# A decoder trunk on one core: 26 weight slots instead of 24, small inputs laid out by the host, and all weights as one array of whole tiles

## The chip, the cores and the metric

The kernel runs on one core of one Trainium2 chip. The metric is the device time of one execution in microseconds (us); lower is better. Three runs of the kernel before took 1004.30, 1004.28 and 1002.66 us (median 1004.28).

## What is computed

Two layers over 256 tokens of width 1024, all in float32. Each layer is a token mixer with a layer norm behind it, then a mixture of experts (MoE) with a layer norm behind it.

```python
for l in range(2):
    parts = split(x @ w_in[l])                       # 3944 columns
    o_a, o_b, o_c = mla(parts), dilated(parts), sparse(parts)
    g = sigmoid(x @ w_gate[l] + b_gate[l])           # 3 branches x 1024
    merged = g[0] * (o_a @ w_a[l]) + g[1] * (o_b @ w_b[l]) + g[2] * (o_c @ w_c[l])
    x = layer_norm(alpha * x + merged @ w_o[l], ln1_g[l], ln1_b[l])
    # one expert group of four per token, then two of its eight experts
    y = sum(combine[:, e:e+1] * ((silu(x @ w1[l][e]) * (x @ w3[l][e])) @ w2[l][e]) for e in range(32))
    x = layer_norm(alpha * x + y, ln2_g[l], ln2_b[l])
```

Each expert has three 1 MB matrices, so the 32 experts of a layer are 96 tiles of 1 MB; the mixer of a layer has 40 tiles, most of them 1 MB.

## The kernel before

**Slots.** SBUF holds NSLOT = 24 slots of 8 KB per partition (1 MB each). Activations and weights share them (class `Slots`). The class `Ring` holds the 272 weight tiles of both layers in the order of their use. `get` hands a tile to the code that uses it, `done` gives its slot back, and at every change of the count `pump` issues as many further tiles as fit: `fits` looks at the log of a dry run of the same program, so that a prefetched tile never takes a slot that an activation needs before the tile is done. Every weight load is issued on SP's queue (`issue`, lines 191 to 198), in the order of the list. Before a load is started, SP waits until the slot's last reader is done; it also waits for the load eight places before it.

**Layout of the weights.** `plan_weights` (L347) cuts the weights into tiles. A whole expert's w1, w3 or w2 lies in HBM as one run of 1 MB, 8 KB per partition. The other tiles are cut out of wider matrices: chunks of w_in with 408 to 512 columns (rows of about 1.6 to 2 KB), gate tiles with 256 columns (rows of 1 KB). In each MoE three kinds of tiles are cut so that work can start before a whole expert is there: w1 of experts 0 to 3 and w3 of experts 28 to 31 by pieces of k (`by_k`; four transfers of 256 KB a tile, rows of 2 KB), and w2 of experts 28 to 31 by columns (512, 256, 256; rows of 2 and 1 KB).

**Small inputs.** `load_small` (L402) fills 59 rows of a 128x128 tile (gains and biases), the router's weights and its bias with eleven transfers on POOL's queue. It runs in `setup` for layer 0 and at the end of the third group of four experts (`e == 2 * Q`) for layer 1. `load_gains` (L448) fetches the two rows of the last norm on POOL's queue in the sixth group (`e == NE - 3 * Q`), and `mixer` fetches `gpk` there too.

**Stages.** `setup` loads x and the first chunks, `make_xT` transposes x (L522). The mixer of a layer is written out by hand in the order of PE. `moe` (L1690 on) takes the experts in eight groups of four: w1 and w3 (both L1708), the gather of the next group (L1667), w2 (L1788), and the combination of the group before (L1774). A group needs twelve tiles, which come in the order w1, w1, w3, w3, w2, w2 of two experts, then the same of the other two:

```python
w = [self.ring.get((l, n, e + i)) for i in range(Q)]
for k in range(KD):
    up(c, k, [w[i][:, k] for i in range(Q)])
```

So the first product of a group waits for the eighth of its twelve tiles. The last group (experts 28 to 31) comes in another order: four w1, four pieces of w3, then w2 by columns. Between its pieces stand short dummy products (`warm`, L294). `spread_gains` (L461) spreads the rows of the last norm in the seventh group.

## Time and profile before

| what | value |
|---|---|
| three runs, median | 1004.28 us |
| the profiled execution | 1004.42 us |
| its span (first to last instruction) | 1002.7 us |
| PE busy | 902.2 us, 90% |
| DVE, ACT, POOL busy | 473.8, 419.0, 165.6 us |
| moved by DMA | 284.76 MB, mean 284 GB/s |
| mean granted clock of PE | 0.954 |

The profiled execution lies 1.7 us above its span and 0.14 us above the median of the runs. Its page gives each engine's busy time; the span in 40 slices of 25 us with each engine's share in tenths, the clock that PE was granted, and the load of the 16 DMA engines; and the chain of waits that ended last. A busy share of 90% is a mean over stages, so the same quantities are then read stretch by stretch.

### The profile page before, as it was taken

What the parts mean: (1) busy time and instruction counts of PE and PEld (TensorE: products, weight loads), DVE (VectorE), ACT (ScalarE), POOL (GpSimd) and SP (SyncE); (2) the same over time, 40 slices, a digit from 0 to 9 for tenths busy, and PEclk for the clock granted to TensorE, in tenths of its full rate; (3) what the DMA queues carried; (4) which work ended last, traced back from release to release, by engine and by line L of the source; (5) the groups of instructions that cost most, each with busy time, mean ns of one, the idle gap of its engine ahead of it and who ended that gap; (6) DMA issues with size and microseconds to landing.
All of it is one profiled execution on the core that took longest, in us unless ns stands there. A gap on an engine that the chain in (4) does not pass through costs nothing.

```text
span 1002.7 us, 18677 instructions
## 1 busy us (share of the span) xinstructions
PE 902.2 (90%) x7584; PEld 706.5 (70%) x7591; DVE 473.8 (47%) x968; ACT 419.0 (42%) x911; POOL 165.6 (17%) x278
## 2 busy tenths in 40 slices
PE   8999999999999966769999999999999997776694
PEld 7888899999985633435489888998999754443251
DVE  5848676945553111111288687676566421100014
ACT  5545555644552301122274646665444632220131
POOL 4531110012100210000035162000451000000001
PEclk9999999999999977789999999999999999987798
DMA  9933171597879999999994044436959899999994
GB/s 330 324 123 126 44 251 43 169 344 244 336 256 404 415 401 419 418 417 396 357 383 139 19 136 149 138 109 217 329 205 401 305 416 417 421 417 419 419 354 150
DMA packets 100170, 284.76 MB, mean 284 GB/s; under 512 B 6324, under 2 KB 53808, under 8 KB 78576
## 3 DMA queue, kind: packets, MB, share of 16 engines
q1 hardware_dynamic: 99088, 283.12, 75.0%
q8 instruction: 62, 1.02, 0.4%
q0 software_dynamic: 992, 0.39, 0.2%
q14 instruction: 28, 0.23, 0.1%
HBM read 282.44 MB, written 1.05 MB: 283 GB/s over the span
## 4 chain that ended last, share of the span: by engine, by line
PE 57%; DMA 25%; issue 8%; POOL 3%; DVE 3%; ACT 2%; SPq 1%; POOLq 0%; DVEq 0%; ACTq 0%
DMA w<-in_w_dram 23%; PE bank L286 12%; PE bank L287 12%; PE bank L288 12%; PE bank L1708 5%; PE bank L840 3%; DMA w<-in_w_in_dram 2%; PE bank L894 2%; PE bank L881 2%; PE bank L1788 2%; PE bank L1667 2%; DVE ws L282 1%; PE bank L843 1%; ACT xp L1443 1%; PE bank L1774 1%
## 5 line engine op out<-in xcount | busy, mean ns | idle before, releaser
L282 DVE TENSOR_TENSOR ws<-w,ws 128x1024 fp32r<-128x1024 f32 (+2 forms) x154 | 190.8, 1248 | 128.3 <-ACT ws L281 123.4
L1708 PE MATMUL bank<-w,xg 128*32 128x256 f32 x2048 | 148.5, 423 | 69.0 <-DMA w<-in_w_dram 59.8
L1708 PEld LDWEIGHTS bank<-w,xg 128*32 128x32 f32 x2048 | 71.0, 121 | 148.3 <-DMA w<-in_w_dram 70.8
L281 ACT ACTIVATE ws<-w 128x1024 fp32r<-128x1024 f32 (+2 forms) x158 | 158.6, 1023 | 35.2 <-PE bank L288 14.4
L286 PE MATMUL bank<-ws,xTh 128*128 128x408 f32 (+3 forms) x320 | 115.9, 362 | 1.2 <-ACT xTh L281 1.2
L286 PE MATMUL bank<-xTh,ws 128*128 128x256 f32 x384 | 111.2, 290 | 0.0
L287 PE MATMUL bank<-ws,xTh 128*128 128x408 f32 (+3 forms) x320 | 110.0, 344 | 1.1 <-POOL ws L282 1.1
L288 PE MATMUL bank<-ws,xTl 128*128 128x408 f32 (+3 forms) x320 | 110.2, 344 | 0.1
L287 PE MATMUL bank<-xTl,ws 128*128 128x256 f32 x384 | 108.6, 283 | 0.0
L288 PE MATMUL bank<-xTh,ws 128*128 128x256 f32 x384 | 108.5, 283 | 0.0
L1738 DVE SCALAR_TENSOR_TENSOR t<-t,cw,bank 128x256 f32<-128x256 f32 x16 | 10.8, 676 | 199.8 <-PE bank L1708 199.8
L1671 ACT ACTIVATE xg<-bank,gpk 128x128 f32<-128x128 f32 x128 | 50.9, 454 | 95.3 <-PE bank L1667 92.7
L286 PEld LDWEIGHTS bank<-xTh,ws 128*128 128x128 f32 x384 | 73.5, 191 | 1.8 <-issue 1.0
L287 PEld LDWEIGHTS bank<-xTl,ws 128*128 128x128 f32 x384 | 73.6, 192 | 0.2
L288 PEld LDWEIGHTS bank<-xTh,ws 128*128 128x128 f32 x384 | 73.5, 191 | 0.0
L1733 ACT ACTIVATE t<-bank 128x256 f32<-128x256 f32 x16 | 6.1, 384 | 146.3 <-PE bank L1708 146.3
L856 ACT ACTIVATE p<-bank,nb 128x128 f32<-128x128 f32 (+1 forms) x92 | 37.3, 420 | 70.0 <-DVE nb L848 65.1
L286 PEld LDWEIGHTS bank<-ws,xTh 128*128 128x128 f32 x320 | 60.9, 190 | 7.7 <-issue 1.7
L1667 PE MATMUL bank<-xg,xp 128*128 128x128 f32 x512 | 63.0, 276 | 2.0 <-ACT xg L1671 2.0
L1667 PEld LDWEIGHTS bank<-xg,xp 128*128 128x128 f32 x512 | 60.6, 192 | 5.9 <-issue 2.5
L287 PEld LDWEIGHTS bank<-ws,xTh 128*128 128x128 f32 x320 | 60.9, 190 | 4.7 <-POOL ws L282 1.4
L288 PEld LDWEIGHTS bank<-ws,xTl 128*128 128x128 f32 x320 | 60.8, 190 | 4.9 <-DVE xTl L282 0.7
(361 smaller groups left out, 1582.2 us busy)
## 6 DMA issues: line engine op xcount, KB each, us to landing
w<-in_w_dram SPq DMA_DIRECT2D x168, 1024.0 KB, 19.0
w<-in_w_gate_dram SPq DMA_DIRECT2D x24, 1024.0 KB, 5.4
w<-in_w_dram SPq DMA_DIRECT2D x80, 256.0 KB, 7.2
w<-in_w_in_dram SPq DMA_DIRECT2D x18, 1024.0 KB, 11.8
w<-in_w_in_dram SPq DMA_DIRECT2D x12, 816.0 KB, 12.8
w<-in_w_o_dram SPq DMA_DIRECT2D x8, 1024.0 KB, 10.0
w<-in_w_a_dram SPq DMA_DIRECT2D x4, 1024.0 KB, 5.4
w<-in_w_c_dram SPq DMA_DIRECT2D x4, 1024.0 KB, 5.3
```

Source lines behind the costliest of these rows:

```text
L281: self.nc.scalar.activation(hi, src, AF.Copy)
L282: (self.nc.gpsimd if self.lo_pool else self.nc.vector).tensor_tensor(lo, src, hi.bitcast(F32), op=ALU.subtract)
L286: m(out, sh, mh, start=start, stop=False)
L287: m(out, sh, ml, start=False, stop=False)
L288: m(out, sl, mh, start=False, stop=stop)
L840: nc.tensor.matmul(b[:, j * w:(j + 1) * w], q[:, blk * P:(blk + 1) * P], k[:, 0:w], start=j == 0, stop=False)
L856: nc.scalar.activation(p[:, j], v[:, j], AF.Exp, bias=nb[:, j:j + 1], scale=u["scale"], accum_out=sm[:, j:j + 1])
L881: nc.tensor.transpose(ps[:, n * P:(n + 1) * P], p[:, j * P:(j + 1) * P], self.ident)
L894: nc.tensor.matmul(ps[half * 64:(half + 1) * 64, pr * P:(pr + 1) * P], u["v"](u["heads"][pr], kb), u["pt"][:, u["pt0"] + pr * nkb + kb], s ...
L1667: nc.tensor.matmul(ps[:, i * P:(i + 1) * P], self.xn[:, t, k + i], pm[:, t, j:j + Q].rearrange("p e c -> p (e c)"), start=t == 0, stop=t = ...
L1671: nc.scalar.activation(xg[:, k + i], ps[:, i * P:(i + 1) * P], AF.Identity, bias=b, scale=g)
L1708: nc.tensor.matmul(hp[i * CAP:(i + 1) * CAP, c * 256:(c + 1) * 256], xg[:, k, i * CAP:(i + 1) * CAP], w[i], start=k == 0, stop=k == KD - 1 ...
```

## The change

- NSLOT goes from 24 to 26. To make room the kernel asks for 64 bytes of scratch for the DMAs that POOL issues, and POOL issues none any more.
- The host writes all 272 weight tiles one behind the other into one array, `stream`, each tile as it lies in SBUF: partition by partition, each partition's bytes in one run of up to 8 KB. Every tile is one transfer. The order of the tiles is the same. w1, w3 and w2 stay as inputs for a path for overfull experts.
- The host lays out the small inputs: `vecs` (128 rows of 128 values, and the router's bias in row 0), `router` and `gpk`. `load_small` makes two transfers in place of eleven, on ACT's queue in `setup` and on SP's queue in the MoE. `gpk` and the rows of the last norm go to SP's queue, one transfer each.
- The rows of the last norm are loaded in the fourth group (`e == 3 * Q`), not in the sixth.

```diff
-NSLOT = 24
+NSLOT = 26
...
+def tiles(l):
...
+    def kp(a, n):
+        return a.reshape(n, P, -1).transpose(1, 0, 2)
...
+    def by_k(n, e0):
+        for k in range(0, KD, 2):
+            yield (l, n, e0, k), [P, Q, 2, DE], lambda a, k=k: np.stack([pk(a[n][l, e], KD)[:, k:k + 2] for e in range(e0, e0 + Q)], 1)
...
+def laid_stream(a):
+    out = np.empty(NSTREAM, np.float32)
+    o = 0
+    for l in range(L):
+        for _, shape, view in tiles(l):
+            n = P * int(np.prod(shape[1:]))
+            out[o:o + n].reshape(shape)[...] = view(a)
+            o += n
+    return out
...
         key, shape, src = self.queue.pop(0)
         t = self.slots.tile(shape, F32, "w")
-        for i, part in enumerate(src if isinstance(src, list) else ()):
-            self.nc.sync.dma_start(t[:, i], part)
-        if not isinstance(src, list):
-            self.nc.sync.dma_start(t, src)
+        self.nc.sync.dma_start(t, src)
...
     def plan_weights(self, l):
...
+        for key, shape, o, n in STREAM:
+            if key[0] == l:
+                src = self.a["stream"][o:o + P * n]
...
+                self.ring.add(key, shape, src.rearrange(pat, p=P, **kw))
...
     def load_small(self, l, home, o):
...
-        v = self.v = self.t([P, P], F32, "vec", 1)
-        nc.gpsimd.memset(v, 0.0)
-        nc.gpsimd.dma_start(v[0:2], a["q_norm_g"][l].rearrange("(k p) -> k p", p=P))
...
-        nc.gpsimd.dma_start(self.wgb[:, :, 40:72], a["w_sub"][l].rearrange("(k p) f -> p k f", p=P))
...
+        eng = nc.sync if l else nc.scalar
+        small = self.t([P, P + 36], F32, "vec", 1)
+        eng.dma_start(small, a["vecs"][l])
+        self.v, self.br = small[:, 0:P], small[0:1, P:P + 36]
         self.wgs = home
...
+        eng.dma_start(home[:, o + KD * 36:o + 2 * KD * 36], a["router"][l])
...
-    def load_gains(self, l, which, rows=P):
+    def load_gains(self, l):
         gb = self.slots.alloc([P, 2, D], F32, "gb")
-        for j, n in enumerate(("g", "b")):
-            self.nc.gpsimd.dma_start(gb[:rows, j], self.a[f"ln{which}_{n}"][l:l + 1].broadcast_to([rows, D]))
+        self.nc.sync.dma_start(gb[:1], self.a["ln2"][l:l + 1])
...
                 self.gpk = self.t([P, 2 * KD], F32, "gpk", 1)
-                for j, n in enumerate(("ln1_g", "ln1_b")):
-                    nc.gpsimd.dma_start(self.gpk[:, j * KD:(j + 1) * KD], self.a[n][l].rearrange("(p k) -> p k", p=P))
+                nc.sync.dma_start(self.gpk, self.a["gpk"][l])
...
-            if e == NE - 3 * Q:
-                self.gb2 = self.load_gains(l, 2, 1)
+            if e == 3 * Q:
+                self.gb2 = self.load_gains(l)
...
-    nc = _bacc.Bacc("TRN2", target_bir_lowering=False, num_devices=1)
+    nc = _bacc.Bacc("TRN2", target_bir_lowering=False, num_devices=1, dynamic_dma_scratch_size=64)
```

The order of PE and DVE is the same in both kernels but for the name of one operand. It differs on the queues, at three places.

**ACT's queue at the start of the program** (`vec` holds gains and biases, `masks` is the slot in which the router's weights wait). Before:

```order
L1361 ACT_TABLE_LOAD
L1361 ACTIVATE dummy_122<-one 128x1
L281 ACTIVATE xTh_124<-bank_126 128x4x128
L281 ACTIVATE xTh_124<-bank_133 128x4x128
L281 ACTIVATE ws_147<-w_84 128x832
```

Now:

```order
L444 DMA vec_108<-in_vecs_dram 128x164
L448 DMA masks_103<-in_router_dram 128x288
L1387 ACT_TABLE_LOAD
L1387 ACTIVATE dummy_111<-one 128x1
L364 ACTIVATE xTh_113<-bank_115 128x4x128
```

The two small loads of layer 0 now stand ahead of ACT's first work; before, POOL issued eleven at that point.

**SP's queue at the start of the mixer of layer 0**, where the first load stands that waits for another engine (DVE, PE) to give a slot back; DMAHW names are the waits for the load eight places before. Before:

```order
L197 DMA w_163<-in_w_in_dram 128x4x408 [waits DMAHW6_49]
L197 DMA w_165<-in_w_in_dram 128x4x512 [waits DMAHW7_49]
L197 DMA w_167<-in_w_in_dram 128x4x512 [waits DMAHW0_49]
L197 DMA w_169<-in_w_in_dram 128x8x256 [waits DMAHW1_49]
L197 DMA w_225<-in_w_in_dram 128x4x512 [waits DMAHW2_49,DVE_49,PE_49]
L197 DMA w_268<-in_w_in_dram 128x4x512 [waits DMAHW3_49,DVE_49]
```

Now:

```order
L280 DMA w_152<-in_stream_dram 128x1632 [waits DMAHW0_49]
L280 DMA w_154<-in_stream_dram 128x2048 [waits DMAHW1_49]
L280 DMA w_156<-in_stream_dram 128x2048 [waits DMAHW2_49]
L280 DMA w_158<-in_stream_dram 128x2048 [waits DMAHW3_49]
L280 DMA w_160<-in_stream_dram 128x2048 [waits DMAHW4_49]
L280 DMA w_162<-in_stream_dram 128x2048 [waits DMAHW5_49]
L280 DMA w_218<-in_stream_dram 128x2048 [waits DMAHW6_49,DVE_49,PE_49]
L280 DMA w_261<-in_stream_dram 128x2048 [waits DMAHW7_49,DVE_49]
```

w_163 and w_152 are the same tile, the tenth. Two more tiles go out ahead of the first that waits for a slot, and the load that waits is the 16th tile instead of the 14th.

**SP's queue in the MoE of layer 0**, where the small loads of layer 1 now stand; `wr` is a slot, the `w` are weight tiles. Before, SP has weight tiles alone there, and POOL has twelve rows, of which these are the first:

```order
L405 MEMSET vec_3908 128x128
L406 DMA vec_3908<-in_q_norm_g_dram 2x128
L407 DMA vec_3908<-in_kv_norm_g_dram 1x16x8
L408 DMA vec_3908<-in_b_gate_dram 24x128
L409 DMA vec_3908<-in_ln_g_dram 8x128
```

Now SP has:

```order
L280 DMA w_3883<-in_stream_dram 128x2048
L280 DMA w_3885<-in_stream_dram 128x2048
L444 DMA vec_3888<-in_vecs_dram 128x164
L448 DMA wr_3887<-in_router_dram 128x288
L280 DMA w_3924<-in_stream_dram 128x2048
L280 DMA w_3926<-in_stream_dram 128x2048
```

The two loads moved from POOL's queue into the row of the weights on SP's. w_3885 is the 97th tile of the layer; the fifth group, whose end uses what `load_small` brought, takes tiles 89 to 100. The rows of the last norm stand in the same way behind the 108th tile.

## Rows read from the trace of the kernel before

**Rows 1.** The page: the span in 40 slices of 25 us.

```profile
PE   8999999999999966769999999999999997776694
PEclk9999999999999977789999999999999999987798
DMA  9933171597879999999994044436959899999994
GB/s 330 324 123 126 44 251 43 169 344 244 336 256 404 415 401 419 418 417 396 357 383 139 19 136 149 138 109 217 329 205 401 305 416 417 421 417 419 419 354 150
```

**Rows 2.** Chain of waits: start us, us, what; both MoE stages.

```profile
321.80 15.23 DMA w<-in_w_dram
337.09 19.88 DMA w<-in_w_dram
...
439.85 12.45 DMA w<-in_w_dram
452.34 5.36 PE bank L1708 x58
...
815.81 16.73 DMA w<-in_w_dram
...
892.44 20.24 DMA w<-in_w_dram
```

**Rows 3.** Timeline of PE, fourth to seventh group of layer 1: start, us, [idle before <-releaser].

```profile
852.53 4.93 PE L1708 MATMUL bank<-w,xg 128*32 128x256 f32 x58 [1.44 <-DMA w<-in_w_dram]
...
942.76 5.88 PE L1708 MATMUL bank<-w,xg 128*32 128x256 f32 x58 [1.43 <-DMA w<-in_w_dram]
949.12 3.66 PE L1708 MATMUL bank<-w,xg 128*32 128x256 f32 x64 [0.47 <-ACT t L1733]
```

**Rows 4.** Stretches: PE, PEld, DVE, ACT, POOL busy; PE's clock, DMA share, GB/s.

```profile
240.00:255.00 15.00, 15.00 (x127) 15.00 (x126) 8.92 (x14) 7.94 (x12) 3.07 (x4) 1.00 0.44 150
735.00:745.00 10.00, 10.00 (x85) 10.00 (x85) 7.39 (x6) 4.66 (x7) 9.20 (x6) 1.00 0.09 38
790.00:795.00 5.00, 4.51 (x71) 2.47 (x69) 0.70 (x2) 3.48 (x9) 0.68 (x2) 1.00 0.42 102
795.00:943.00 148.00, 110.77 (x1170) 63.60 (x1174) 24.03 (x40) 31.86 (x82) 4.82 (x8) 0.89 1.01 418
940.00:945.00 5.00, 3.30 (x26) 1.28 (x30) 0.00 (x0) 0.00 (x0) 0.00 (x0) 0.50 1.01 419
```

**Rows 5.** Layer 1, fourth group: PE's wait for its seventh tile.

```profile
850.03 1.06 PE L1708 MATMUL bank<-w,xg 128*32 128x256 f32 x2 [4.58 <-DMA w<-in_w_dram]
```

**Rows 6.** SP's queue, 300 to 452 us: waited for, us in total, times, longest.

```profile
SPq L197 <- DMA w<-in_w_dram: 94.1, 45, 3.7
SPq L197 <- PE bank L1708: 14.3, 6, 5.8
```

**Rows 7.** Stretches of DMA at the end of layer 1.

```profile
970.00:978.00 8.00, 7.84 (x81) 3.45 (x81) 0.00 (x0) 1.57 (x3) 0.00 (x0) 1.00 1.00 348
979.00:984.00 5.00, 4.14 (x18) 0.66 (x16) 0.42 (x1) 0.00 (x0) 0.00 (x0) 1.00 1.09 351
```

**Rows 8.** Timeline of PE, last group of layer 0: w2 by columns.

```profile
490.48 1.92 PE L1788 MATMUL bank<-w,t 128*32 128x512 f32 x16 [0.52 <-DVE t L275]
492.33 0.60 PE L294 MATMUL bank<-mk 128*128 128x512 bf16 x2
492.87 1.07 PE L1788 MATMUL bank<-w,t 128*32 128x256 f32 x16
...
496.61 1.39 PE L1774 MATMUL bank<-y,t 128*128 128x256 f32 x8
```

**Rows 9.** The same of layer 1.

```profile
979.76 2.12 PE L1788 MATMUL bank<-w,t 128*32 128x512 f32 x6 [0.52 <-DVE t L275]
982.20 1.90 PE L1788 MATMUL bank<-w,t 128*32 128x512 f32 x10 [0.32 <-DMA w<-in_w_dram]
...
989.34 1.36 PE L1774 MATMUL bank<-y,t 128*128 128x256 f32 x8
```

**Rows 10.** Start of the program: timeline of PE and of ACT, and two stretches.

```profile
5.62 1.06 PE L522 MATMUL bank<-cst,x 128*128 128x128 f32 x8 [0.80 <-DMA x<-in_x_dram]
9.44 1.09 PE L522 MATMUL bank<-cst,x 128*128 128x128 f32 x8 [1.89 <-DMA x<-in_x_dram]
...
6.28 1.08 ACT L281 ACTIVATE xTh<-bank 128x512 fp32r<-128x512 f32 x2 [4.02 <-PE bank L522]
...
10.00:12.00 2.00, 2.00 (x14) 1.98 (x13) 1.97 (x3) 1.09 (x2) 0.00 (x0) 1.00 1.06 208
12.00:25.00 13.00, 13.00 (x71) 12.68 (x70) 8.72 (x9) 7.96 (x11) 3.28 (x5) 1.00 1.05 387
```

**Rows 11.** Layer 0: a stretch; PE behind the spread gains in layers 0 and 1.

```profile
355.00:360.00 5.00, 1.06 (x2) 0.18 (x2) 0.00 (x0) 0.00 (x0) 0.41 (x1) 0.68 1.04 338
...
477.00:478.00 1.00, 1.00 (x14) 0.43 (x8) 0.00 (x0) 0.00 (x0) 0.00 (x0) 0.50 0.93 342
475.00 5.35 PE L1708 MATMUL bank<-w,xg 128*32 128x256 f32 x64
...
965.97 3.66 PE L1708 MATMUL bank<-w,xg 128*32 128x256 f32 x64
```

More of the change, by code (lines that the diff above doesn't have):

```diff
@@ new lines, in stream @@
+def stream():
+    o, out = 0, []
+    for l in range(L):
+        for key, shape, _ in tiles(l):
+            n = int(np.prod(shape[1:]))
+            out.append((key, shape, o, n))
+            o += P * n
+    return out, o
+STREAM, NSTREAM = stream()
+def laid_stream(a):
+    out = np.empty(NSTREAM, np.float32)
+    o = 0
+    for l in range(L):
+        for _, shape, view in tiles(l):
[3 more added lines that the diff above has]
+    return out
@@ L347, in plan_weights @@
     def plan_weights(self, l):
-        a, r = self.a, self.ring
-        kp = "(k p) f -> p k f"
-        def win(c):
-            _, c0, w = CHUNKS[c]
-            if w > 256:
-                for h in range(2):
-                    r.add((l, "in", c, h), [P, 4, w], a["w_in"][l, h * 512:(h + 1) * 512, c0:c0 + w].rearrange(kp, p=P))
-            else:
-                r.add((l, "in", c, 0), [P, 8, w], a["w_in"][l, :, c0:c0 + w].rearrange(kp, p=P))
-        for c in range(3):
-            win(c)
@@ L374, in plan_weights @@
-        for h in range(2):
-            r.add((l, "w_o", 0, h), [P, 4, 512], a["w_o"][l, h * 512:(h + 1) * 512, 0:512].rearrange(kp, p=P))
-        for c in (1, 2):
-            c0, w = WO[c]
-            r.add((l, "w_o", c), [P, 8, w], a["w_o"][l, :, c0:c0 + w].rearrange(kp, p=P))
-        pk = "(p k) f -> p k f"
-        def by_k(n, e0):
-            for k in range(0, KD, 2):
-                r.add((l, n, e0, k), [P, Q, 2, DE], [a[n][l, e].rearrange(pk, p=P)[:, k:k + 2] for e in range(e0, e0 + Q)])
@@ L385, in plan_weights @@
-        by_k("w1", 0)
-        for e in range(0, NE - Q, 2):
-            for n in ("w1", "w3") if e >= Q else ("w3",):
-                for i in range(2):
-                    r.add((l, n, e + i), [P, 8, DE], a[n][l, e + i].rearrange(pk, p=P))
-            for i in range(2):
-                r.add((l, "w2", e + i), [P, 2, D], a["w2"][l, e + i].rearrange("(p j) f -> p j f", p=P))
-        for e in range(NE - Q, NE):
-            r.add((l, "w1", e), [P, 8, DE], a["w1"][l, e].rearrange(pk, p=P))
@@ L394, in plan_weights @@
[L394 to L399 removed]
+        for key, shape, o, n in STREAM:
+            if key[0] == l:
+                src = self.a["stream"][o:o + P * n]
+                pat = "(p a) -> p a" if len(shape) == 2 else f"(p {' '.join('abc'[:len(shape) - 1])}) -> p {' '.join('abc'[:len(shape) - 1])}"
+                kw = {c: d for c, d in zip("abc", shape[1:])} if len(shape) > 2 else {}
+                self.ring.add(key, shape, src.rearrange(pat, p=P, **kw))
@@ L442, in small_rows @@
         for k in range(KD):
-            nc.tensor.matmul(ps[:, 0:72], self.one.broadcast_to([P, P]), self.wgb[:, k], start=k == 0, stop=False)
+            nc.tensor.matmul(ps[:, 0:72], self.one.broadcast_to([P, P]), self.wgb[:, :, k], start=k == 0, stop=False)
         nc.tensor.matmul(ps[:, 36:72], self.one[0:1].broadcast_to([1, P]), self.br, start=False, stop=True)
@@ L1939, with laid_out @@
     Trunk(tc, ctx, a, out, dbg, (dry.slots.log, dry.ring.ends)).run()
-_INS = ["x", "w_in", "q_norm_g", "w_uq", "kv_norm_g", "w_ukv", "w_gate", "b_gate", "w_a", "w_b", "w_c", "w_o",
-        "ln1_g", "ln1_b", "w_group", "b_group", "w_sub", "b_sub", "w1", "w3", "w2", "ln2_g", "ln2_b"]
+_INS = ["x", "w1", "w3", "w2"]
+def laid_out(a):
+    vecs = np.zeros((L, P, P + 36), np.float32)
+    for l in range(L):
+        m = max(l - 1, 0)
+        rows = [a["q_norm_g"][l], a["kv_norm_g"][l], a["b_gate"][l], a["ln1_g"][l], a["ln1_b"][l], a["ln2_g"][m], a["ln2_b"][m]]
+        v = np.concatenate([r.reshape(-1, P) for r in rows])
+        vecs[l, :len(v), :P] = v
+        vecs[l, 0, P:P + 4], vecs[l, 0, P + 4:] = a["b_group"][l], a["b_sub"][l]
+    router = np.concatenate([a["w_group"], a["w_sub"]], 2).reshape(L, KD, P, 36).transpose(0, 2, 1, 3).reshape(L, P, KD * 36)
+    gpk = np.concatenate([a[n].reshape(L, P, KD) for n in ("ln1_g", "ln1_b")], 2)
+    return {"vecs": vecs, "router": router, "gpk": gpk, "ln2": np.stack([a["ln2_g"], a["ln2_b"]], 1)}
 def kernel(**inputs):
```

89 lines of the change are left out of this document (53 added, 36 removed).

## The prediction, made before the changed kernel ran

> **What bounds the kernel now.** Read the 40 slices first [rows 1]. In both mixers (slices 3 to 8 and 22 to 28 above all) PE stands at 9 while the DMA line has low digits: PE sets the time and the weights come with room to spare. In the MoEs (slices 15 to 18 and 34 to 38) it is the other way: DMA at 9 and 401 to 419 GB/s, PE at 6 and 7, its clock line mostly at 7 and 8. The chain of waits says the same: from 321.80 us to 452.34 in layer 0 and from 815.81 to 912.7 in layer 1 it runs through weight loads, and behind that through PE [rows 2].
>
> The timeline of PE shows how such a wait looks. The first product of a group waits for the eighth of the group's twelve tiles. Between the same point of the fourth and the seventh group of layer 1 lie 942.76 - 852.53 = 90.23 us and 36 tiles: **2.51 us a tile of 1 MB**, the 418 GB/s that the stretch has at a DMA share of 1.01 [rows 3, 4]. PE needs less for a group, so until the seventh group its pace doesn't matter: what counts is how far the loads are ahead when the DMA engines become busy for good, at about 300 and 795 us. Just before, they idle: share 0.42 from 790 to 795, 0.09 from 735 to 745, 0.44 from 240 to 255 [rows 4]. There the loads wait for slots, not for bandwidth. From 452.34 and 942.76 on PE works without a long wait to the end of the MoE; that is the seventh group's rest and the eighth.
>
> **The change part by part.** All sums are against the profiled execution, 1004.42 us; the runs' median is 0.14 lower.
>
> *Two slots.* The order on SP's queue shows that two more tiles go out before the first that waits for a slot, and the tile numbers stay shifted by two into the MoE. The idle DMA time can carry them: 10 us at 0.09 leave 9.1, 15 us at 0.44 leave 8.4, and two tiles need 5.0 [rows 4]. So when the DMA engines become busy for good, they are two tiles further, and the eighth tile of the seventh group lands 2 x 2.51 = 5.0 us earlier. PE is there in time: it waited 4.58 us and 1.44 more already in the fourth group of layer 1 [rows 3, 5], so 5.0 leave about 1 us of that wait; the loads stay in front there, and the wait in the seventh group moves by the full 5.0. **Minus 5.0 us in each layer, minus 10.0.** Bounds: 8 (some of a wait turns into PE's own pace) and 10.2.
>
> *The early rows of the last norm* hold a slot from the fourth to the sixth group, where the lead is one tile instead of two. The DMA engines are busy there anyway with eight loads in flight, and SP waits mostly for those (94.1 us) and little for PE (14.3) [rows 6]. Cost 0; without that cover it would be one tile, 2.5 us.
>
> *The layout, at the end of layer 1.* Of the last 16 tiles eight are whole and eight cut: four of w3 by k and four of w2 by columns, rows of 2 and 1 KB in transfers of 256 or 512 KB. The cut ones move at 348 and 351 GB/s where the DMA share is 1.00 and 1.09 [rows 7], against 418. PE feels it at the w2 pieces alone: from the first of them to the last combination layer 0 takes 496.61 - 490.48 = 6.13 us and layer 1 989.34 - 979.76 = 9.58, same instructions, same clock, though the row of waits names only 0.32 us [rows 8, 9]. In layer 0 the pieces were there; in layer 1 they were late by **3.4 us**. Will they be there now? At 2.51 us a tile, counted from the eighth tile of the seventh group, the 14th, 15th and 16th land after 35.1 (the second of the first piece's two tiles), 37.7 and 40.2. PE asks for the first at 979.76 - 942.76 = 37.0 and, at layer 0's pace (492.87 - 490.48 = 2.39 for the next), at 39.4 and about 41.9. Room of 1.7 us each: minus 3.4. Bounds 0 (the rows stay slow) and 3.45.
>
> [...] I go by the rows, since a share of 1.09 at 351 GB/s is an engine that is busy and yet slow [rows 7].
>
> *The layout elsewhere* (gates, w_o, w_in, the first w1 of each MoE): these load while PE sets the time, so nothing; their cover is PE's 15.00 of 15 us busy with DMA at 0.44 [rows 4]. If the cover were gone, one such tile costs about 0.4 us more than a whole one (1.05 MB at 351 or 418).
>
> *The start.* PE waits 0.80 us for the first half of x and 1.89 for the second, which stands behind an 832 KB chunk of w_in in SP's queue [rows 10]. Chunks of that cut move at 387 GB/s, and at 208 while the router's weights come in pieces of 128 and 16 B [rows 10]. Both go. But ACT's two small loads (128x164 and 128x288 values, 0.08 and 0.15 MB) now come in the first microsecond, ahead of most of x: 0.23 MB at 387 is 0.6 us. What the trace can bound is a gain of 1.89 (that wait gone) and a loss of 0.6. I take **minus 1.0**, nearer to the gain, because less is moved in small pieces and PE has nothing else to wait for there. ACT issues them in the 4.02 us that it waits for PE [rows 10].
>
> *Small loads in the MoE.* POOL's eleven transfers for layer 1 are the one thing that I find for the drop to 338 GB/s from 355 to 360 us: 5 x (1 - 338/418) = 0.96 us [rows 11]. The same data in two loads take 0.23 MB at 418 = 0.55. **Minus 0.3**, bounds 0 and 0.9. On SP they stand after the 97th tile, and PE needs them behind the 100th: no wait. `gpk` and the norm's rows are one load each with more than a group of lead: 0. POOL's freed time (eleven issues) hides beside its idle time: 0.
>
> *What stays.* The products behind each wait run at the lower clock, 0.50 from 940 to 945: 5.88 us at first, 3.66 for as many right behind [rows 3, 4]. The order of PE doesn't change, and a dip to 0.50 in layer 0 behind the spread gains makes the first product of the last group 5.35 us long, against 3.66 in layer 1 [rows 11]. Whether that comes again is open: 1.7 us either way.
>
> **Sum:** 10.0 + 3.4 + 1.0 + 0.3 = 14.7; 1004.42 - 14.7 = 989.7, and on the runs' scale **989.6 us**.
>
> **The rivals.**
> 1. *The size of the rows doesn't matter*, and the last tiles of layer 1 are slow for another reason that stays, such as what the other engines do in that stage. Then the gains of 3.4 and 1.0 are lost: 994.0. Against it: a share above 1 at 351 GB/s [rows 7]. For it: small rows, short transfers and the last group come together, so the rows can't tell them apart. [...]
> 2. *The lead doesn't come*, because the ring fills its two slots and then loses them (the norm's rows, the small loads in SP's queue) before the DMA engines are busy for good. Then 4.7 us are left at most: 999.6. Against it: the idle DMA time and the order.
> 3. *Slower: the one array reads more slowly.* All of the DMA-bound time, 300 to 452 and 795 to 943, goes through it. Each percent of rate costs 3.0 us there, so from 14.7/3.0 = 4.9% down (below 398 GB/s) the kernel is slower than before. At the 387 GB/s that cut chunks reach [rows 10] it is 8%, 24 us, 1013.8. Against it: a whole expert already is one run of 1 MB, read at 418, in either layout. For it: nothing that I see, but no row reads all weights from one array.
> 4. *It changes nothing that shows*: if the planner gave the two slots to nothing and the layout lay hidden, 1004.3. The order says otherwise.
>
> **How the numbers follow.** Chance 0.77 for the forecast, 0.11, 0.06, 0.05 and 0.01 for the rivals. The forecast's own bounds are 1004.3 - (10.2 + 3.45 + 1.9 + 0.9 + 1.7) = 986.1 and 1004.3 - (8 + 3.4 - 0.6 - 1.7) = 995.2, with no gain from the small loads; rival 1 lies within. The range is 986 to 995.5; rivals 2 to 4 are left out. A measurement of this kernel can tell about 0.2%, 2 us. Faster by more: 0.93; within: 0.02; slower: 0.05.
>
> **What would show it.** In the changed profile: the eighth tile's wait in the seventh group ends 5 us earlier after its MoE begins, in both layers; in the fourth group the wait is nearly gone; 418 GB/s holds to the last load of layer 1, and the stretch from the first w2 piece to the last combination falls from 9.58 to about 6.1 us; PE's second transposes start about a microsecond earlier; no row below 400 GB/s where the share is above 1. The prediction is wrong if the DMA-bound stretches run below 410 GB/s, if SP waits for PE there longer than its loads in flight last, or if PE's clock is low in places where it was full.

## The result, and the profile of the changed kernel

The change makes the kernel faster: 990.85 us (median of four runs, 985.84 to 993.13) against 1003.97, a ratio of 0.9865 with the interval 0.9821 to 0.9909. Measured again beside the last experiments it took 992.36 us against 1003.05, a ratio of 0.9891 (0.9858 to 0.9924). The profiled execution took 985.84 us, span 984.1. It is the shortest of all ten runs of this kernel, so its trace shows more gain (18.6 us of span) than the medians do (13.1 and 10.7). Where the rest goes is shown below.

The page's slices, to be held against [rows 1]: PE, PE's granted clock, DMA, GB/s.

```profile
PE   8999999999999995769989999999999999776594
PEclk9999999999999997789999999999999999977798
DMA  9933161486888999999993034425849799999993
GB/s 368 383 128 129 44 257 44 154 361 220 326 309 341 421 421 419 419 421 421 419 419 121 26 130 143 158 71 221 347 165 422 286 406 421 419 421 419 421 420 140
```

The shape is the same; what changed is the level. The first slices move 368 and 383 GB/s where 330 and 324 stood, and the two DMA-bound stretches hold 419 to 421 to their last slice, where layer 1 before ended on 354. The timeline of PE gives the places (start, us, [idle before <-releaser]); the first two lines are the kernel before, the rest is the changed one:

```profile
298.07 3.66 PE L1708 MATMUL bank<-w,xg 128*32 128x256 f32 x64
790.99 3.66 PE L1708 MATMUL bank<-w,xg 128*32 128x256 f32 x64
...
9.27 1.09 PE L549 MATMUL bank<-cst,x 128*128 128x128 f32 x8 [2.00 <-DMA x<-in_x_dram]
...
296.42 3.66 PE L1734 MATMUL bank<-w,xg 128*32 128x256 f32 x64
...
444.06 5.44 PE L1734 MATMUL bank<-w,xg 128*32 128x256 f32 x58 [1.42 <-DMA w<-in_stream_dram]
...
466.83 3.66 PE L1734 MATMUL bank<-w,xg 128*32 128x256 f32 x64
...
486.75 1.39 PE L1800 MATMUL bank<-y,t 128*128 128x256 f32 x8
...
781.24 3.66 PE L1734 MATMUL bank<-w,xg 128*32 128x256 f32 x64
...
837.32 3.64 PE L1734 MATMUL bank<-w,xg 128*32 128x256 f32 x58 [1.61 <-DMA w<-in_stream_dram]
...
928.14 5.74 PE L1734 MATMUL bank<-w,xg 128*32 128x256 f32 x58 [1.42 <-DMA w<-in_stream_dram]
...
951.21 3.66 PE L1734 MATMUL bank<-w,xg 128*32 128x256 f32 x64
...
964.99 1.92 PE L1814 MATMUL bank<-w,t 128*32 128x512 f32 x16 [0.52 <-DVE t L358]
...
971.13 1.39 PE L1800 MATMUL bank<-y,t 128*128 128x256 f32 x8
```

L1734 is the line of w1 and w3 (L1708 before), L1814 that of w2, L1800 the combination. 298.07 and 790.99 are the first products of the two MoEs before, 296.42 and 781.24 those now; 444.06 and 928.14 are the products behind the eighth tile of the seventh group. Stretches (PE, PEld, DVE, ACT, POOL busy; clock, DMA share, GB/s):

```profile
10.00:12.00 2.00, 2.00 (x14) 1.98 (x13) 1.89 (x3) 1.57 (x3) 0.00 (x0) 1.00 1.02 423
...
300.00:444.00 144.00, 113.40 (x1189) 66.81 (x1185) 24.92 (x43) 32.08 (x82) 5.49 (x9) 0.91 1.01 418
785.00:928.00 143.00, 109.29 (x1166) 63.39 (x1166) 24.27 (x40) 32.05 (x82) 3.71 (x6) 0.91 1.01 418
...
960.14:964.14 4.00, 3.86 (x40) 1.37 (x40) 0.66 (x1) 0.00 (x0) 0.00 (x0) 1.00 0.99 412
...
967.14:968.14 1.00, 1.00 (x18) 0.42 (x16) 0.53 (x1) 0.44 (x1) 0.00 (x0) 1.00 0.00 0
```

Cut at these points, the two profiled executions compare so:

| stretch | before, us | after, us | difference | predicted |
|---|---|---|---|---|
| start to the second transposes | 9.44 | 9.27 | -0.17 | -1.0 |
| to MoE 0's first product | 288.63 | 287.15 | -1.48 | 0 |
| to the 8th tile of its seventh group | 154.27 | 147.64 | -6.63 | -5.3 |
| to its last combination | 44.27 | 42.69 | -1.58 | open, 1.7 either way |
| to MoE 1's first product | 294.38 | 294.49 | +0.11 | 0 |
| to the 8th tile of its seventh group | 151.77 | 146.90 | -4.87 | -5.0 |
| to its last combination | 46.58 | 42.99 | -3.59 | -3.4 |
| to the end of the span | 13.36 | 12.97 | -0.39 | 0 |

The sum is -18.60 against the predicted -14.7. Four things were open: which edit brings which gain, why MoE 0 and its mixer gained more than predicted, why the start did not, and why the runs scatter over 7 us and more.

### The profile page after: what moved, and what is told of

Same layout as the page of the kernel before. It is cut to its first block, busy times and chain, and to the rows that moved or that the text cites. A ratio compares the mean times of both kernels' runs of the same rounds, so it can differ in the third digit from the quotient of the medians.

```text
span 984.1 us, 18539 instructions
## 1 busy us (share of the span) xinstructions
PE 892.6 (91%) x7584; PEld 704.7 (72%) x7591; DVE 472.2 (48%) x968; ACT 418.5 (43%) x911; POOL 147.9 (15%) x246
## 3 DMA queue, kind: packets, MB, share of 16 engines
q8 instruction: 62, 1.02, 0.4%
HBM read 282.55 MB, written 1.05 MB: 288 GB/s over the span
## 4 chain that ended last, share of the span: by engine, by line
PE 57%; DMA 29%; issue 6%; POOL 4%; ACT 2%; DVE 1%; SPq 0%; POOLq 0%; DVEq 0%; ACTq 0%
DMA w<-in_stream_dram 29%; PE bank L369 13%; PE bank L370 13%; PE bank L371 13%; PE bank L1734 4%; PE bank L867 3%; PE bank L921 2%; PE bank L908 2%; PE bank L1693 1%; PE bank L1814 1%; PE bank L870 1%; ACT xp L1469 1%; POOL t L776 1%; DMA x<-in_x_dram 1%; PE bank L1496 1%
## 5 line engine op out<-in xcount | busy, mean ns | idle before, releaser
L365 DVE TENSOR_TENSOR ws<-w,ws 128x1024 fp32r<-128x1024 f32 (+2 forms) x154 | 188.8, 1236 | 128.1 <-ACT ws L364 124.2
L1734 PE MATMUL bank<-w,xg 128*32 128x256 f32 x2048 | 142.9, 411 | 61.5 <-DMA w<-in_stream_dram 52.3
L1734 PEld LDWEIGHTS bank<-w,xg 128*32 128x32 f32 x2048 | 69.6, 118 | 136.6 <-DMA w<-in_stream_dram 62.7
```

Of the source, the lines that this page charges most:

```text
L365: (self.nc.gpsimd if self.lo_pool else self.nc.vector).tensor_tensor(lo, src, hi.bitcast(F32), op=ALU.subtract)
L1734: nc.tensor.matmul(hp[i * CAP:(i + 1) * CAP, c * 256:(c + 1) * 256], xg[:, k, i * CAP:(i + 1) * CAP], w[i], start=k == 0, stop=k == KD - 1 ...
```

## The experiments

**24 slots, all else as in the change.**

```diff
-NSLOT = 26
+NSLOT = 24
```

> The change with 24 slots in place of 26, everything else kept. My theory (two slots are two tiles of 2.51 us in each MoE): the eighth tile of the seventh group lands 5 us later after its MoE begins, at about 152.6 us in layer 0 (147.6 with 26 slots) and 151.8 us in layer 1 (146.8); the fourth groups' waits come back to about 6 us; the stretch from the first w2 piece to the last combination of layer 1 stays at 6.1 us. The whole kernel takes about 10 us more than with 26 slots: 996 against a profiled 985.8, or 998 if the clock dip behind the spread gains of layer 0 comes back too. The mixer of layer 0 has no theory yet: it became 1.5 us shorter. If that is the layout or the small loads, MoE 0 begins at 296.4 as with 26 slots; if it is the slots, at 297.9. Rival (the one array itself reads faster, the slots do nothing): the eighth tiles stay at 147.6 and 146.8, the total at 986 to 988.

997.21 us median (993.8 to 1000.15), ratio to the kernel before 0.9918 (0.9888 to 0.9948). In the trace, 998.4 us long and that of the longest of these runs, the eighth tiles land 152.44 and 151.05 us after their MoEs begin (449.68 behind 297.24, and 942.30 behind 791.25): 4.8 and 4.2 us later than with 26 slots. So the two slots are worth nearly what two tiles of 2.51 us should be, and the rival falls. The waits of the fourth groups come back, too: 4.00 and 1.86 us in layer 0, 4.03 and 1.42 in layer 1. The medians show less than the 9.0 us of the traces: 997.21 against 990.85, or against the 992.36 measured later, is 6.4 or 4.9 us. MoE 0 begins 287.40 us behind the second transposes, as in the change: the mixer's 1.4 us do not come from the slots. The end of layer 1, timeline of PE:

```profile
942.30 5.90 PE L1734 MATMUL bank<-w,xg 128*32 128x256 f32 x58 [1.42 <-DMA w<-in_stream_dram]
...
979.31 1.92 PE L1814 MATMUL bank<-w,t 128*32 128x512 f32 x16 [0.52 <-DVE t L358]
...
985.44 1.39 PE L1800 MATMUL bank<-y,t 128*128 128x256 f32 x8
```

985.44 - 979.31 = 6.13 us: with 24 slots, too, the w2 pieces are there in time once they are laid out.

**26 slots and the small inputs, but cut weights.** `plan_weights` and `issue` are those of the kernel before:

```diff
-        self.nc.sync.dma_start(t, src)
+        for i, part in enumerate(src if isinstance(src, list) else ()):
+            self.nc.sync.dma_start(t[:, i], part)
+        if not isinstance(src, list):
+            self.nc.sync.dma_start(t, src)
```

> 26 slots and the small inputs laid out, but the weights cut out of their own arrays as in the kernel before (rows of 1, 1.6 and 2 KB, four transfers for a tile by k). My theory (row size, at the end of layer 1 and in the mixers): the last w2 pieces are late again, 9.6 us from the first of them to the last combination where the layout gives 6.1; DMA below 355 GB/s in that stretch; the eighth tiles stay where 26 slots put them, within 1 us; the start of MoE 0 goes back by up to 1.5 us. Total 985.8 + 3.4 + 1.5 = 990.7. Rival 1 (row size doesn't matter): 6.1 us, 418 GB/s, total 986 to 987. Rival (the slots' gain was the layout's): the eighth tiles go back by 5 us each, total near 1000.

989.41 us median (988.35 to 995.2), ratio 0.9868 (0.9822 to 0.9914): the same as the change. The eighth tiles land at 147.61 and 146.82 us, as with the layout. MoE 0 begins 287.17 us behind the second transposes: the mixer's gain is not the layout's either. And the end of layer 1 takes 6.13 us, not 9.6. Stretches behind the eighth tile, and PE:

```profile
949.32:953.32 4.00, 4.00 (x31) 1.73 (x33) 1.84 (x3) 1.19 (x2) 0.00 (x0) 1.00 0.94 319
...
965.32:969.32 4.00, 3.34 (x28) 0.83 (x21) 1.08 (x2) 0.00 (x0) 0.00 (x0) 1.00 1.10 348
...
970.07:971.07 1.00, 1.00 (x17) 0.37 (x10) 0.69 (x1) 0.06 (x2) 0.00 (x0) 1.00 0.22 75
971.07:972.39 1.32, 1.32 (x7) 0.76 (x5) 0.80 (x3) 0.35 (x1) 0.00 (x0) 1.00 0.00 0
```

```profile
952.04 5.35 PE L1783 MATMUL bank<-w,xg 128*32 128x256 f32 x64
...
967.51 1.93 PE L1863 MATMUL bank<-w,t 128*32 128x512 f32 x16 [0.52 <-DVE t L361]
...
973.64 1.39 PE L1849 MATMUL bank<-y,t 128*128 128x256 f32 x8
```

The loads are as slow as in the kernel before (319 and 348 GB/s at shares of 0.94 and 1.10, [rows 7]); no wait shows. They run out over the last 2 us and end at 971.07, 41.75 us behind the eighth tile at 929.32; in the change they end at 967.14, 39.0 us behind it. PE asked for the last piece at 972.39, 43.1 us behind the tile, where the product at 952.04 had run 1.7 us longer (5.35 in place of 3.66, at a granted clock of 0.50 from 954 to 956 us); without that it would have been 41.4, an estimate, and 0.3 us too early. So the cut tiles do cost 2.7 us of DMA, but with 26 slots PE, in this trace, hides them.

**The size of the rows alone.** The last eight cut tiles of layer 1 lie in the array as four or eight pieces, one transfer a tile:

```diff
+                if cut(key):
+                    self.ring.add(key, shape, src.rearrange("(q p a) -> p q a", q=pieces(key), p=P))
+                    continue
```

> The change, but the eight cut tiles at the end of layer 1 (w3 by k, w2 by columns) lie in the one array as 4 or 8 pieces behind each other, so that each tile is still one transfer of 1 MB but is read in rows of 2 KB (w3 and the first w2 columns) or 1 KB (the others) in place of 8 KB. My theory (row size): DMA at about 350 GB/s for the pieces with 1 KB rows, 350 to 390 for those with 2 KB, the stretch from the first w2 piece to the last combination of layer 1 at 8.5 to 9.6 us, total 2.4 to 3.4 us above the change: 988 to 989 against 985.8. Rival (it was the short transfers of 256 KB, or the strided reads of w2 in HBM): 418 GB/s, 6.1 us, total as the change.

993.5 us median (988.45 to 995.27), ratio 0.9878 (0.9831 to 0.9925): no difference to the change that the runs can show. The rates are what the theory said:

```profile
956.05:960.05 4.00, 4.00 (x33) 1.58 (x36) 0.00 (x0) 0.60 (x1) 0.00 (x0) 0.50 1.05 387
...
966.00:970.00 4.00, 3.92 (x40) 1.35 (x39) 0.00 (x0) 0.00 (x0) 0.00 (x0) 1.00 1.07 354
```

387 GB/s for rows of 2 KB, 354 where those of 1 KB come, 412 to 424 for 8 KB in the same stage of the change: the size of the rows alone makes the loads slower, with the share at 1.05 and 1.07. From the first w2 piece to the last combination it is 6.11 us, not the 8.5 to 9.6 that I expected: the clock at 0.50 in the first of these rows made PE late by more than the loads were. From the eighth tile to the last combination it is 47.05 us, 4.1 more than in the change, and layer 0, where no tile is changed, has 46.57, 3.9 more.

**Short transfers with long rows.**

```diff
+        for p in range(0, P, 32) if cut(key) else ():
+            self.nc.sync.dma_start(t[p:p + 32], src[p:p + 32])
```

> The change, but the same eight tiles are read in four transfers of 256 KB, 32 partitions each, with rows of 8 KB. My theory (row size): no loss from the shorter transfers, 418 GB/s, 6.1 us from the first w2 piece to the last combination of layer 1, total as the change. Rival (short transfers were slow, since only eight loads are in flight and each waits for the load eight places before): about 350 GB/s, 9.6 us, total 3.4 us above the change. A loss here could also come from the few partitions of a transfer, a gain or a zero could not.

1005.96 us median (1003.51 to 1013.45), 15 us slower than the change. A tile in four transfers of 32 partitions moves at 240 and 221 GB/s, against 412 to 424 in the same stage of the change:

```profile
952.00:956.00 4.00, 4.00 (x33) 1.58 (x36) 0.00 (x0) 0.60 (x1) 0.00 (x0) 0.50 0.94 240
...
960.00:964.00 4.00, 3.70 (x39) 1.26 (x38) 0.00 (x0) 0.25 (x2) 0.00 (x0) 1.00 1.01 221
```

That answers another question than I asked: with the DMA share at 0.94 and 1.01 the engines are busy, so it isn't the wait for the load eight places before, and the few partitions of a transfer are what is left of the two losses that I named. Whether short transfers over all partitions cost anything is left open by it. (The cut tiles by k, 256 KB over 128 partitions, move at 274 to 322 GB/s at the end of layer 1 in the four traces that have them there, against 387 for rows of that size in one transfer. That may be the short transfers, or that these rows don't lie side by side in HBM; no run tells the two apart.)

**The last norm's rows at their old place.**

```diff
-            if e == 3 * Q:
+            if e == NE - 3 * Q:
                 self.gb2 = self.load_gains(l)
```

> The change, but the last norm's two rows are loaded at the end of the sixth group, as in the kernel before, so that their slot is taken two groups later. My theory (in the fourth and fifth group the loads wait for loads, not for slots): no difference, the eighth tile of the seventh group within 0.5 us of 147.6 and 146.9 us after its MoE begins, total as the change. Rival (a slot less is a tile less of lead): it lands 2.5 us earlier, total 5 us less than the change.

1015.9 us median (1015.16 to 1016.31), ratio 1.0123 (1.0087 to 1.0160), 25 us slower than the change. Neither theory: the eighth tiles land at 147.78 and 147.04 us, so the slot costs nothing, as I said. But what was not costed is the place in SP's queue. The view of the tile `gb`, and PE in layer 0:

```profile
L479 SPq DMA_DIRECT2D gb<-in_ln_dram x2: 274/286/298, 459.4 to 958.6; - x2
```

```profile
472.45 7.16 PE L488 MATMUL bank<-gb,one 1*128 1x512 f32 x8 [9.01 <-DMA gb<-in_ln_dram]
479.54 6.40 PE L1734 MATMUL bank<-w,xg 128*32 128x256 f32 x64
```

The program issues the load at the end of the sixth group, but SP runs through a queue with the weights fetched ahead in front of it, and gets there only at 459.4 us, in the seventh (in the change: at 395.4). PE's wait ends 13 us after that; on POOL's queue, in the kernel before, the rows were issued at 440.8 us and landed some 5 us later. PE waits 9.01 us, and the products behind the wait take nearly twice as long (7.16 us in place of 3.69, then 6.40 in place of 3.66). So the move to the fourth group is what makes the move from POOL's queue to SP's possible.

**The small inputs alone.** The first try had 24 slots, cut weights, and the rows of the last norm at their old place, on SP's queue:

> The kernel before (24 slots, weights cut out of their own arrays, last norm's rows in the sixth group) with the small inputs alone laid out by the host and loaded by ACT and SP. My theory: the 1.4 us that the mixer of layer 0 became shorter belong to the small loads, since they came with 24 slots and with the cut weights as well. From the second transposes to the first product of MoE 0 then 287.2 us (288.6 before). Part of MoE 0's gain belongs to them too: the eighth tile of the seventh group 152.4 us after MoE 0 begins (154.3 before), and at 151.0 to 151.8 in layer 1. The end of layer 1 stays 9.6 us from the first w2 piece to the last combination. Total 1004.4 - 1.4 - 1.9 - 0.4 = 1000.7. Rival (each of the other two parts brought the 1.4 by itself): 288.6, 154.3, total 1004.

1026.21 us (1023.54 to 1026.82), where I expected 1000.7: the wait just shown, in both layers. What precedes it can be read: the eighth tiles land at 152.05 and 152.41 us, and the mixer of layer 0 takes 288.93 us, as the rival says. With the rows in the fourth group:

```diff
-            if e == NE - 3 * Q:
+            if e == 3 * Q:
```

> The kernel before with the small inputs laid out and on ACT's and SP's queues, and the last norm's rows in the fourth group: 24 slots and cut weights stay. In the study before this one the rows stood in the sixth group on SP's queue, where they came behind the weights fetched ahead, and PE waited 8 to 10 us for them in each layer; that is taken away here. My theory: the mixer of layer 0 loses POOL's wait of 1.3 us (287.2 us from the second transposes to MoE 0, or up to 1.6 more if the clock dips at the start), the eighth tile of the seventh group lands 152.2 us after MoE 0 begins (154.3 before) and 151 to 152.4 in layer 1; the last combination of layer 1 comes 46 us or more behind the eighth tile (46.6 before, 43.0 after the change). Total 1004.4 - 1.4 - 2.1 = 1001, within 2. Rival (slots or layout are needed for that, too): 1004.

1001.64 us median of ten (1000.94 to 1005.33), ratio 0.9989 (0.9968 to 1.0010): by the medians 1.4 us, and no difference that is certain. Two stretches, and PE at the end of layer 1:

```profile
10.00:14.00 4.00, 4.00 (x18) 3.84 (x17) 3.25 (x5) 2.77 (x4) 0.00 (x0) 0.62 1.06 383
...
355.00:360.00 5.00, 1.69 (x10) 0.58 (x14) 0.00 (x0) 0.00 (x0) 0.00 (x0) 0.57 1.01 419
```

```profile
979.07 1.92 PE L1863 MATMUL bank<-w,t 128*32 128x512 f32 x16 [0.52 <-DVE t L361]
...
986.14 1.36 PE L1849 MATMUL bank<-y,t 128*128 128x256 f32 x8
```

First, the drop to 338 GB/s [rows 11] is gone: 419. The eighth tile of MoE 0 lands at 153.13 (152.05 in the try before) where it was 154.27: the small loads are worth 1.1 to 2.2 us there. Layer 1, which has none, comes 0.7 later than the 151.77 of the kernel before (152.49 and 152.41), so these figures are no sharper than that.

Second, the mixer of layer 0 takes 288.73 us here and not 287.2; but the clock is at 0.62 from 10 to 14 us, which costs 1.5 (in the first try 0.59 and 1.6; both are estimates), and PE's wait of 1.26 us for POOL's `cs` in the kernel before is absent here as in every other kernel with these loads off POOL. Where that wait came from stands in the trace of the kernel before (the line at 11.47 is the change's):

```profile
13.14 1.69 ACT L281 ACTIVATE ws<-w 128x832 fp32r<-128x832 f32 x2 [1.92 <-DMA w<-in_w_in_dram]
39.59 0.46 POOL L749 TENSOR_TENSOR t<-pjC,cst 128x128 f32<-128x128 f32 x1 [2.16 <-DVE pjC L275]
48.34 0.33 PE L1015 MATMUL bank<-cst,cs 128*128 128x128 f32 x1 [1.26 <-POOL cs L990]
...
11.47 1.69 ACT L364 ACTIVATE ws<-w 128x832 fp32r<-128x832 f32 x2 [0.43 <-DMA w<-in_stream_dram]
```

ACT could start on the second chunk of w_in only 3.70 us behind the second transposes, in the change 2.20, after a stretch in which the DMA moved 208 GB/s [rows 10] and not 423. DVE, which works on the same chunks behind ACT, gave POOL its `pjC` 30.15 us behind the second transposes, in the change 28.71. POOL itself had issued its last small load by 8.6 us and sat idle for 2.16 us before that. So the mixer's 1.4 us are for the most part that wait, and it comes from the small loads by way of the DMA, not from POOL's time. The chain is read from the waits; no run takes one link of it alone.

Third, the end of layer 1 takes 7.07 us with cut rows and 24 slots, both as before, 0.94 late in place of 3.44. The last combination comes 43.65 us behind the eighth tile there, not the 46 or more that I expected.

This run completes a square of four kernels, all with the small inputs laid out and the norm's rows in the fourth group (medians, ratios to the kernel before):

| | 24 slots | 26 slots |
|---|---|---|
| cut weights | 1001.64 (0.9989) | 989.41 (0.9868) |
| whole tiles | 997.21 (0.9918) | 990.85 (0.9865), 992.36 (0.9891) |

The slots bring 12.2 us with cut weights, and 4.9 to 6.4 with whole tiles; whole tiles bring 4.4 with 24 slots, and nothing with 26. The intervals are 2 to 4 us either way, so the sizes are rough, but the two gains don't add up, and the prediction added them.

**The start.**

```diff
-        eng = nc.sync if l else nc.scalar
+        eng = nc.sync
```

> The change, but the two small loads of layer 0 are issued on SP behind the masks in place of ACT's queue in the first microsecond. My theory of the missing gain at the start (the two loads, 0.23 MB, share the DMA engines with x and so give back 0.6 us): PE's second transposes at 8.6 to 8.9 us in place of 9.27, and ACT's table load at once. Rival (x waits for the chunk of w_in ahead of it and for its own landing, and the start scatters by itself: 9.27, 9.66, 9.81, 9.84 and 10.39 in five kernels with the same first loads): anywhere between 9.2 and 10.4. Total within 1 us of the change in either case.

991.33 us median (985.62 to 994.29), ratio 0.9891 (0.9848 to 0.9933), as the change. The second transposes start at 9.00 us, within neither of the two ranges; in the twelve other traces with the loads off POOL they start between 8.73 and 10.39. The wait for x stays:

```profile
9.00 1.09 PE L549 MATMUL bank<-cst,x 128*128 128x128 f32 x8 [1.29 <-DMA x<-in_x_dram]
```

A gain of 0.3 us or none; one trace can't tell it from the scatter.

**Dummy products in the wait.**

```diff
                     w = [self.ring.get((l, n, e + i)) for i in range(Q)]
+                    if (e, c) == (NE - 2 * Q, 0):
+                        self.warm(32, self.mk)
```

> The change, with 32 dummy products (some 7 us at full clock) ahead of the seventh group's first product, in which PE waits 8.7 us and then 1.4 us for weights. My theory of the spread among runs and of the 5.4 to 5.9 us that the first products behind that wait take, where the same number takes 3.64 us at full clock: PE is granted half its clock because it stood idle. With dummy products in the wait the products behind it run at full clock (3.64 us, 1.8 to 2.1 us less in each layer), and the product behind the spread gains is 3.66 us in both layers; total 981.5 to 983 against 985.8 for the change's best run, and a narrower spread among runs. Rival (the clock falls for another reason, such as the load of the DMA engines or of PE itself): 5.4 us as before and the same total; or slower by what the dummy products take at half clock beyond the wait, up to 6 us a layer.

989.39 us median (986.23 to 992.37), ratio 0.9863 (0.9818 to 0.9908): no gain over the change, and runs as far apart. PE:

```profile
467.18 5.35 PE L1734 MATMUL bank<-w,xg 128*32 128x256 f32 x64
...
930.55 3.64 PE L1734 MATMUL bank<-w,xg 128*32 128x256 f32 x58 [1.88 <-DMA w<-in_stream_dram]
...
952.35 5.35 PE L1734 MATMUL bank<-w,xg 128*32 128x256 f32 x64
```

Half right. In layer 1 the product behind the wait takes 3.64 us, as at full clock, against 5.74, in layer 0 it takes 4.92, from 444.92 on. But the product behind the spread gains is slow in both layers (5.35 in place of 3.66). So filling the wait does not remove that second dip, not even in layer 1, where there was none behind the wait; it stands behind the spread gains, products that read a single row of `gb`.

**The change once more.** No edit.

> The changed kernel once more, beside the next two. Its runs scattered from 985.8 to 993.1. My theory: the scatter is TensorE's clock in the seventh and eighth group of each layer, where PE sets the time: from the eighth tile of the seventh group to the last combination the kernels so far took 42.7 to 47.7 us with the same instructions, by how many of the products there fell on a stretch at half clock. Expected: runs again from 985 to 994; in the profiled one the two stretches explain the difference to 985.84 within 1.5 us. Rival (the DMA rate or the start differ from run to run): the eighth tiles land at other times than 147.6 and 146.9 us after the MoEs begin, or the second transposes begin more than 2 us later.

992.36 us median (987.23 to 996.05). The profiled run, 987.23 us, PE and a stretch:

```profile
466.42 5.35 PE L1734 MATMUL bank<-w,xg 128*32 128x256 f32 x64
...
950.95 5.35 PE L1734 MATMUL bank<-w,xg 128*32 128x256 f32 x64
```

```profile
466.00:472.00 6.00, 6.00 (x67) 2.98 (x66) 0.36 (x1) 0.69 (x2) 0.00 (x0) 0.72 1.01 416
```

The same 64 products took 3.66 us in both layers of the first trace. From the eighth tile to the last combination it is 43.94 and 44.09 us against 42.69 and 42.99, together +2.35, and the eighth tile of layer 1 lands 1.02 earlier; the spans differ by 1.4. Over all traces with this order of PE, and no wait for loads in it, that stretch takes from 42.7 to 47.1 us, and the row of the clock (0.72) shows what differs. It fits the scatter of the runs. The longest of them, 996.05, has no trace, but a run of 993.81 us has one, that of the kernel with the small rows: its two stretches (46.57 and 47.05) are together 7.9 us longer than those of the first trace, and its span 8.0.

**The spread gains moved into the wait.**

```diff
+            if e == NE - 3 * Q:
+                self.spread_gains(self.gb2)
             if e == NE - 2 * Q:
-                self.spread_gains(self.gb2)
```

> The change, with the spreading of the last norm's rows moved from the end of the seventh group to the end of the sixth, ahead of PE's long wait for the seventh group's weights. The eight spread products (3.7 us at full clock) read one row each; behind them the product of the last group took 5.35 to 6.6 us in some traces and 3.66 in others. My theory: in the wait of 8.7 us the spreading costs nothing, and 3.7 us of PE leave the stretch from the eighth tile to the last combination; but the last tiles then land no earlier than 39 us after the eighth, so the stretch falls from 42.7 to 43.0 us in the change's best run only to about 41, and a dip of the clock there hides behind the loads. Total 985.84 - 2 x 1.9 = 982, with runs within 4 us of each other. Rival 1 (the loads stay hidden): 39.2 us for the stretch, total 978.5. Rival 2 (the dip comes from the wait, not from the spread products, or the evacuations of the spread rows delay the group): as the change, 986 to 993, or slower.

984.02 us median (982.1 to 984.36), ratio to the kernel before 0.9804 (0.9775 to 0.9832): 8.3 us below the change on the same chip, whose interval (0.9858 to 0.9924) lies above, and the runs lie within 2.3 us of each other. PE in layer 0:

```profile
431.83 3.70 PE L488 MATMUL bank<-gb,one 1*128 1x512 f32 x8
...
440.71 1.06 PE L1734 MATMUL bank<-w,xg 128*32 128x256 f32 x2 [4.63 <-DMA w<-in_stream_dram]
443.20 5.62 PE L1734 MATMUL bank<-w,xg 128*32 128x256 f32 x58 [1.42 <-DMA w<-in_stream_dram]
...
463.25 3.64 PE L1734 MATMUL bank<-w,xg 128*32 128x256 f32 x58 [0.24 <-DMA w<-in_stream_dram]
...
478.52 1.91 PE L1814 MATMUL bank<-w,t 128*32 128x512 f32 x12 [0.45 <-DMA w<-in_stream_dram]
...
484.84 1.39 PE L1800 MATMUL bank<-y,t 128*128 128x256 f32 x8
```

The spreading now stands in the wait, which shrinks from 8.73 to 4.63 us. The stretch from the eighth tile to the last combination is 41.64 and 41.02 us, the 41 of the theory, and PE waits for loads there again (0.24 and 0.45 us in layer 0; in layer 1 the sixteen products of the first w2 piece take 2.94 us at full clock, in place of 1.92), so that rival 1 falls. In layer 1 the eight products in the wait ran at a granted clock of 0.73 and took 4.63 us, and PE still waited 2.59 us behind them: that dip cost nothing. Of the 8.3 us, 3.7 are there in the best case (982.1 against 985.84); the rest fits the scatter that is gone: the granted clock is 1.00 in the last group of both layers (460 to 470 and 945 to 956 us).

**Both moves.**

> The kernel with the spreading moved, and the two small loads of layer 0 on SP behind the masks (alone they brought the second transposes from 9.27 to 9.00 us in one look). My theory: the sum of both, 0.3 us below the kernel with the spreading alone, which a median of its runs can't show. Rival: the start scatters by itself, transposes anywhere from 9.0 to 10.4.

982.56 us median (981.04 to 983.83), ratio 0.9788 (0.9762 to 0.9814), the second transposes at 9.10. The fastest median of all, though its interval overlaps that of the kernel with the spreading alone.

## Why the prediction was right, and where it was not

The time and its sign came out: 990.85 us lies 1.3 above the 989.6 and well inside 986 to 995.5. The slots are the main cause, as predicted. That the figure is so close is in part luck: the profiled execution gained 3.9 us more than the sum, the clock of the other runs took that back, and the sum holds 3.4 us for a layout that the kernel with 26 slots does without. By its steps:

- **Two slots, minus 10.0: right in the traces.** 24 slots in the changed kernel cost 4.8 and 4.2 us to the eighth tiles; of the medians' difference, 4.9 to 6.4 us, less is certain. In layer 1 the fourth group's waits fell from 4.58 and 1.44 us [rows 3, 5] to 1.61 and 0.21, where about 1 was to be left. Rival 2 falls.
- **The early norm rows, 0: right for the slot, and short-sighted.** The place matters for another reason, SP's queue: two groups later the same load makes the kernel 25 us slower. The prediction named the lead of these loads ("more than a group"), but not that the move made it necessary.
- **The layout at the end of layer 1, minus 3.4: right in the sum, wrong as a term.** The stretch fell by 3.44 us, and the slow rows exist (354 to 387 GB/s against 418 and more). But the step "8th tile plus so many slow tiles against PE's demand" took the 9.58 us of one trace as what cut rows cost. With cut rows it takes 6.13 us behind 26 slots, and 7.07 behind 24. So of the 3.4 us 0.9 are the cut tiles' in the one trace with 24 slots, and with 26, where PE was held up by its clock, none (0.3 by the estimate at full clock). That the term came out is luck. Why the cut tiles of the kernel before came 2.5 us later still is not settled; its DMA moved 274 to 285 GB/s at a place where the others with cut tiles moved 311 to 322, and what still differs is the loads on POOL's queue and the place of the norm's rows.
- **Rival 1** gave 994.0 by losing the layout. The kernel without the layout took 989.41, so for the time of this kernel the size of the rows hardly mattered, though for the DMA rate it did. The rival was right that the end of layer 1 does not hang on the size of the rows here, and wrong that it stays slow: it shrank without the layout.
- **The start, minus 1.0: failed as to the place.** At the second transposes it was 0.17, less than the scatter there (8.73 to 10.39 us). The rate rose as said (208 [rows 10] to 423 GB/s from 10 to 12 us), but x had landed by then. What failed is the step "PE has nothing else to wait for there": ACT, DVE and POOL handed the slow stretch on to PE's wait of 1.26 us for `cs`, at 48.34 us.
- **The layout elsewhere and POOL's freed time, 0: right as far as the runs show.** The 1.48 us that the mixer of layer 0 gained come with whole and with cut weights, so they are not the layout's, and POOL sat idle ahead of the chain that came late. They are the start's, in another place.
- **Small loads in MoE 0, minus 0.3: mis-sized.** They measure 1.1 to 2.2. The drop (0.96 us) was read rightly, as far as one can say beside a scatter of 0.7 to 1.0; the 0.55 us given back for the new loads can't be seen.
- **What stays, 1.7 either way: too narrow.** The clock in the last two groups moves a run by up to 4.4 us in each layer. That fits the 18.6 us of the best run beside the 13.1 of the median; the other three runs beside it have no trace.
- **Rival 3** falls: 418 GB/s from one array in both stretches.

## What to carry to other kernels

A load moved to a queue that prefetches is issued where the queue stands, not where the program stands (here at 459.4 us, where POOL's queue had it at 440.8): count what is ahead of it, and issue small loads as many groups earlier. A late load seen in one trace is a difference between two clocks, that of the loads and that of the consumer (9.58 us in one trace, 7.07 and 6.13 in two others with the same cut rows), so a term read from it is only as good as the consumer's pace; test it with the cause undone. Work that PE does behind its last long wait is worth moving into the wait, here 8 us for one moved call, also because a dip of its clock there cost nothing (4.63 us in place of 3.7, with 2.59 us of waiting left). And two changes that give the loads more lead cover the same waits (the two slots brought 12.2 us with cut weights, 4.9 to 6.4 with whole tiles): add up their gains only after a run with each alone.

## What was not expected of the hardware

Loads over 32 of the 128 partitions, rows of 8 KB, moved 215 to 240 GB/s at DMA shares of 0.93 to 1.02, against 418 at a share of 1.01 over all partitions. What holds them there no run shows.

PE's granted clock fell with the engine busy. From 10 to 14 us it was 0.62 and 0.59 in two traces and 1.00 in the other twelve, at the same work. In the last group it fell to 0.50 in 11 of the 20 layers of ten traces, during or right behind eight products that each read a single row, and not in the others; with those products moved away the clock was 1.00 there in both layers of both traces. Whether these products bring the dip about is not shown: the same edit moves the place where it would fall, and four layers are few.
